# Attention inside a two-layer streaming encoder: two heads' value products issued together on the two column halves of the array, a mask added by strips, new keys kept in the middle of each cache block, and the query latent normalised step by step

## The chip, the core and the metric

The kernel runs on one core of one Trainium2 chip. A core has a matrix engine (PE, with its weight loads listed as PEld), a vector engine (DVE), a scalar or activation engine (ACT), a general engine (POOL) and a queue engine that issues transfers (SP). The metric is the device time of one execution in microseconds (us). Times given for a kernel are medians of the runs shown; the profile is one execution more.

## The reference, cut to what matters

One inference step of an encoder with two trunk layers. Layer 0 mixes a gated linear recurrence with a gated linear attention; layer 1 is a multi-head latent attention (16 heads); each is followed by a SwiGLU feed-forward. There are 256 prompt positions and 8 running streams of 16 new positions each, so 384 columns in all. The change lies in layer 1:

```python
cq, ckv, kpe = split(u @ w_in, [384, 640])
q = (rms_norm(cq, q_norm) @ w_uq).reshape(B, L, 16, 96)      # 64 plain + 32 rotary
# prompt: keys and values are expanded from ckv, block-causal mask over chunks of 64
s = (q_nope @ k_nope + q_pe @ kpe) * SM_SCALE
s = where(key_chunk <= q_chunk, s, -inf);  o = softmax(s) @ v
# samples: 512 cached latents and 16 new ones for each stream
c_all = concat([cache_ckv, ckv]);  k_all = concat([cache_kpe, kpe])
s = (q_lat @ c_all + q_pe @ k_all) * SM_SCALE
o_lat = softmax(s) @ c_all;  o = o_lat @ w_uv
```

All inputs and outputs are float32.

## The kernel before

Activations lie transposed: features on the 128 partitions, the 384 positions (256 prompt, 8 x 16 sample) along the free axis. Most products are made of three matmuls on operands split into a high and a low part (`mm3`, L287 to L289); the parts are of a rounded 32-bit type, with one matmul instruction each. Products of plain float32 operands appear in the trace as two passes, so two PE instructions for one call. Transposes are one pass.

Weights and the samples' caches come as a stream of chunks of 128 x 1024 floats (the caches' transposed chunks, `cT`, have 1056 columns). Each is loaded (L98), copied to a high part on ACT (L110), and its low part is made on DVE (L126) and partly on POOL (L121). The order of the work is the order of the code: the schedule is written out by hand, every engine takes its instructions in order, and waits are set where data needs them.

PSUM (the banks that matmuls write) is dealt out as two rings: six banks `mm` and two `sd`, each given out in turn. A matmul into a bank waits until the previous content has been read.

Layer 1 has four stretches:

- *Query latent.* Six tiles of `cq`, `kpe`, `ckv` come out of one group of matmuls into the six `mm` banks. For each of the three `cq` tiles in turn: DVE scales it (L1129), ACT squares it for the norm (L327, L333, L335), ACT makes the high part with the gain (L311), and DVE makes the low part (L312). Then three heads' queries are computed (the `uq` group, L287 to L289, 27 matmuls, into the first three `mm` banks again), the sums of squares are made (L342, L344) and turned into the two factors (L348, L350), and a matmul with `sel` gathers the rotary key (L1165, in an `sd` bank). The squares of `ckv` (first L327, in the same accumulator tile as those of `cq`) stand ahead of the queries in ACT's order. The normalised `ckv` (L1171) is split into `ckr`, which the values' matmuls read (L297 to L299).
- *Prompt attention.* A loop over ticks t = -1 to 19. In a tick stand, in this order: keys of a pair of heads (odd ticks, `a_keys`), one head's queries (most ticks), the transposes of head t-2 (`a_trans`, L1231), the division of head t-1 (`a_norm`), the value product of head t-3 (`a_value`, L1238 to L1240), the scores of head t (`a_score`). In `a_score` a matmul of the identity with the mask (L1209, 384 columns) opens the sum, and the query-key products follow (L1210, L1211). `a_value` has three products of 128 columns with a stationary tile of 64 columns; even heads write partitions 0 to 63 and odd heads 64 to 127 of a shared bank, in different ticks. After the odd head the pair is copied out (L1243, L1244). In the last ticks, units of the samples' latent queries (L1264, L1401) stand beside it.
- *Sample attention.* A loop over the 8 streams, with the softmax of one beside the products of the one before. Keys are 512 cached ones and 16 new ones, which stand after the cached ones for even streams and ahead of them for odd ones. For stream b the scores of two head groups come in two halves of 264 columns (L1325 to L1328). The probabilities are transposed: four transposes for each group (`trans`, L1353), and in `trans_rest` the 32 columns around the new keys, by a matmul with a stationary tile of 32 columns that writes 32 partitions (L1362). `value` multiplies with the cached latents (four tiles, L287 to L289) and, last, with the new ones: only the 32 partitions `r` that hold the pair of streams, in both operands (shape 32*128), twice in each stream (`ct` = 0 and 1). The rotary keys' cache is loaded by L1284 and split by L1299 (ACT) and L1300 (POOL).
- *Latent to output, output projection, feed-forward*, not touched.

Of the kernel before, what the change touches and what calls it, by code (L numbers as in the profile page):

```python
# [176 lines left out]
def emit(ctx, tc, A, O):  # L177
# [1021 lines left out]
    pair = {}  # L1199
# [7 lines left out]
    def a_score(h, ps):  # L1207
        q, k = qp[:, h % NQ, :], kst[:, h % 4, :]
        pe.matmul(ps, idr, amr, start=True, stop=False)  # L1209
        pe.matmul(ps[:, 0:P], q[:, 0:P], k[:, 0:P], start=False, stop=False)  # L1210
        pe.matmul(ps[:, P:T], q[:, P:TP], k, start=False, stop=True)  # L1211
        mx = small([P, 3], "mx")
        v_.reduce_max(mx, ps.rearrange("p (a b) -> p a b", b=P), axis=AX.X)
        v_.tensor_max(mx[:, 1:2], mx[:, 1:2], mx[:, 2:3])
        v_.tensor_scalar(mx[:, 0:2], mx[:, 0:2], -SM_SCALE, None, op0=OP.mult)
        pr = prb[:, h % 4, :]
        l = small([P, 2], "sl")
        s_.activation(pr[:, 0:P], ps[:, 0:P], AF.Exp, scale=SM_SCALE, bias=mx[:, 0:1], accum_out=l[:, 0:1])
        s_.activation(pr[:, P:T], ps[:, P:T], AF.Exp, scale=SM_SCALE, bias=mx[:, 1:2], accum_out=l[:, 1:2])
        return l  # L1220
# [13 lines left out]
    def a_value(h):  # L1234
        e, pt = h % 2, ptb[:, h % 4, :]
        ps = pair[h // 2][64 * e:64 * e + 64]
        va, vb = vp[0][:, h * 64:h * 64 + 64], vp[1][:, h * 64:h * 64 + 64]
        pe.matmul(ps[:, 0:P], va, pt[:, 0:P], start=True, stop=True)  # L1238
        pe.matmul(ps[:, P:TP], va, pt[:, P:TP], start=True, stop=False)
        pe.matmul(ps[:, P:TP], vb, pt[:, TP:T], start=False, stop=True)  # L1240
        if e:
            hi, lo = oh_at(h // 2), ol_at(h // 2)
            s_.activation(hi[:, 0:TP], pair[h // 2], AF.Copy)  # L1243
            v_.tensor_sub(lo[:, 0:TP], pair.pop(h // 2), f(hi)[:, 0:TP])  # L1244
# [26 lines left out]
    HK = NKEY // 2  # L1271
    HALF = 512

# [3 lines left out]
    def new_at(b):  # L1277
        return slice(0, NS) if b % 2 else slice(PAST, NKEY)

    def past_at(b):  # L1280
        return slice(NS, NKEY) if b % 2 else slice(0, PAST)

    def b_load(b):
        nc.sync.dma_start(krb[b % 2][:, past_at(b)], A["ckpe"][b])  # L1284

    def b_new(b):
        ns = slice(TP + b * NS, TP + (b + 1) * NS)
        c = N_W1 + max(2 * b - 1, 0)
        if c in S.raw:
            pairs = [(S.raw[c], ckv)]  # L1290
        else:
            pairs = [(x, f(ckr)[:, p_]) for p_, x in enumerate(S.parts[c])]
        for x, src in pairs:
            g_.tensor_copy(x.rearrange("p (c k) -> p c k", c=2)[:, :, new_at(b)], src[:, :, ns])
        g_.tensor_copy(krb[b % 2][:, new_at(b)], kper[0:96, ns])
# [6 lines left out]
    class Sample:  # L1302
# [4 lines left out]
        def __init__(self, b):  # L1307
            self.b, self.sc, self.mx, self.l = b, {}, {}, {}
            self.pr = [tmp([P, NS + NKEY]) for _ in range(2)]
            z = 0 if b % 2 else NKEY  # L1310
            for pr in self.pr:
                g_.memset(pr[:, z:z + NS], 0.0)

        def score(self, hg, hi, lo, between=None):
# [3 lines left out]
            self.sc[hg] = [mm(HK) for _ in range(2)]  # L1318
            for e, sc in enumerate(self.sc[hg]):
                if e and between:  # L1320
                    between()
                es = slice(e * HK, (e + 1) * HK)
# [13 lines left out]
        def soft(self, hg):  # L1336
            mx, l, pr = self.mx[hg], small([P, 2], "sls"), self.pr[hg]
            o = NS * (self.b % 2)
            for e in range(2):
                s_.activation(pr[:, o + e * HK:o + (e + 1) * HK], self.sc[hg][e], AF.Exp, scale=SM_SCALE,  # L1340
                              bias=mx[:, 0:1], accum_out=l[:, e:e + 1])
            self.l[hg] = l
# [14 lines left out]
        def trans_rest(self):  # L1357
            self.trans(1)
            r, c0 = rows(self.b), PAST * (1 - self.b % 2)
# [6 lines left out]
        def value(self, hi, lo):  # L1366
            r = rows(self.b)
            self.o = mm(512).rearrange("p (c t) -> p c t", c=2)
            ch, cl = (x.rearrange("p (k c) -> p k c", c=256) for x in (hi, lo))
            for ct in range(2):  # L1370
# [4 lines left out]
                x = tuple(z[r, 4].rearrange("p h t -> p (h t)") for z in (pt_hi, pt_lo))  # L1375
                mm3(self.o[:, ct], (cnew[0][r, cs], cnew[1][r, cs]), x, False, True)
# [35 lines left out]
    for t in range(-1, H_C + 4):  # L1412
        if t % 2:
            if t + 1 < H_C:
                a_keys((t + 1) // 2, mm(TP))
            pair[(t - 3) // 2] = mm(TP)
# [12 lines left out]
        if 0 <= t - 3 < H_C:  # L1429
            a_value(t - 3)  # L1430
# [39 lines left out]
    pt_lo = slot(2, [P, 5, 2, P], F32R, name="pt_lo")  # L1470
    prev = None
# [76 lines left out]
def _pack(inputs):  # L1548
# [67 lines left out]
    ct[0::2, ..., :PAST], ct[1::2, ..., NS:] = cp[0::2], cp[1::2]  # L1616
# [82 lines left out]
```

## Time and profile before

| | |
|---|---|
| median of 3 runs | 1168.84 us (1166.83 to 1172.54) |
| the profiled execution, its time | 1170.78 us |
| the profiled execution, first to last instruction | 1169.0 us |
| busy PE | 1122.6 us (96%), 6627 instructions |
| busy DVE | 673.2 us (58%) |
| busy ACT | 541.8 us (46%) |
| busy POOL | 216.9 us (19%) |
| mean granted TensorE clock | 0.982 of full |

Shares of busy time are means over stages with different limits. A matmul record lasts longer than the time until the next one can start, since matmuls are pipelined; what a matmul costs in a dense stretch is the distance from its start to the next start. A row of the timeline that ends in x4 holds four instructions in a row; brackets give the idle time of the engine ahead of it and what ended it.

### The profile page before, as it was taken

The numbers are of one execution on the slowest core, as the hardware profiler recorded it, in microseconds if no ns is written. First come the engines' busy times: TensorE is split into PE (matmuls) and PEld (weight loads), VectorE is DVE, ScalarE is ACT, GpSimd is POOL, SyncE is SP. The second block draws the span as 40 slices with busy tenths as digits, with TensorE's granted clock in tenths as the row PEclk, the third lists the DMA queues.
The fourth block names the chain that finished last, engine by engine and source line by source line (L and its number), as shares of the span: only waits on it lengthen the run. The fifth ranks groups of instructions, "written<-read, shape, count | busy, mean of one in ns | idle before, by whom it ended". The sixth has DMA issues, their size and how long they took to land.

```text
span 1169.0 us, 16900 instructions
## 1 busy us (share of the span) xinstructions
PE 1122.6 (96%) x6627; PEld 1079.9 (92%) x6627; DVE 673.2 (58%) x1046; ACT 541.8 (46%) x924; POOL 216.9 (19%) x248
## 2 busy tenths in 40 slices
PE   8976999999999999999999899899999999999995
PEld 8976888999999999999999798699899999999995
DVE  5779666856447655553225677677437655554223
ACT  5534485255445433333334566567555433333331
POOL 4178253100112000000102121155212000000102
PEclk9988899999999999999999999999999999999998
DMA  7312247534433333443433251334333433333331
GB/s 260 110 55 66 80 144 241 175 106 168 127 93 122 129 127 127 126 127 126 125 128 98 90 163 55 110 113 134 98 109 108 139 123 124 124 125 124 126 108 54
DMA packets 41745, 142.80 MB, mean 122 GB/s; under 512 B 4833, under 2 KB 7137, under 8 KB 41665
## 3 DMA queue, kind: packets, MB, share of 16 engines
q1 hardware_dynamic: 39744, 135.92, 36.3%
q0 software_dynamic: 1488, 5.31, 1.1%
q8 instruction: 52, 0.85, 0.3%
q10 hardware_dynamic: 432, 0.49, 0.1%
q14 instruction: 29, 0.23, 0.1%
HBM read 134.82 MB, written 6.88 MB: 121 GB/s over the span
## 4 chain that ended last, share of the span: by engine, by line
PE 88%; DVE 7%; ACT 2%; issue 1%; POOL 1%; DMA 1%; SPq 0%; DVEq 0%; ACTq 0%
PE mm L287 25%; PE mm L289 24%; PE mm L288 24%; DVE xc L695 2%; PE mm L297 1%; PE mm L299 1%; PE mm L298 1%; DVE wlo L126 1%; PE sd L530 1%; PE mm L1325 1%; PE mm L1326 1%; PE mm L1327 1%; PE mm L877 1%; PE sd L1353 1%; DMA wraw<-wst 1%
## 5 line engine op out<-in xcount | busy, mean ns | idle before, releaser
L126 DVE TENSOR_TENSOR wlo<-wraw,whi 128x1024 fp32r<-128x1024 f32 (+1 forms) x232 | 278.2, 1200 | 285.8 <-ACT whi L110 285.6
L110 ACT ACTIVATE whi<-wraw 128x1024 fp32r<-128x1024 f32 (+1 forms) x232 | 244.4, 1054 | 232.2 <-PE mm L289 207.7
L287 PE MATMUL mm<-uhi,whi 128*128 128x384 f32 x1016 | 347.2, 342 | 4.2 <-ACT uhi L311 4.1
L289 PE MATMUL mm<-ulo,whi 128*128 128x384 f32 x1016 | 345.3, 340 | 0.8 <-DVE ulo L312 0.8
L288 PE MATMUL mm<-uhi,wlo 128*128 128x384 f32 x1016 | 344.3, 339 | 0.6 <-DVE wlo L126 0.6
L287 PEld LDWEIGHTS mm<-uhi,whi 128*128 128x128 f32 x1016 | 193.0, 190 | 5.5 <-ACT uhi L311 5.0
L289 PEld LDWEIGHTS mm<-ulo,whi 128*128 128x128 f32 x1016 | 192.2, 189 | 1.9 <-DVE ulo L312 1.9
L288 PEld LDWEIGHTS mm<-uhi,wlo 128*128 128x128 f32 x1016 | 192.1, 189 | 1.2 <-DVE wlo L126 1.1
L336 POOL TENSOR_TENSOR acc<-acc,sq 128x384 f32<-128x384 f32 x49 | 59.9, 1222 | 683.1 <-ACT sq L335 682.5
L287 PE MATMUL mm<-ah,whi 128*128 128x384 f32 x352 | 118.9, 338 | 0.0
L289 PE MATMUL mm<-al,whi 128*128 128x384 f32 x352 | 118.9, 338 | 0.0
L288 PE MATMUL mm<-ah,wlo 128*128 128x384 f32 x352 | 118.6, 337 | 0.0
L287 PEld LDWEIGHTS mm<-ah,whi 128*128 128x128 f32 x352 | 66.3, 188 | 0.0
L289 PEld LDWEIGHTS mm<-al,whi 128*128 128x128 f32 x352 | 66.1, 188 | 0.0
L288 PEld LDWEIGHTS mm<-ah,wlo 128*128 128x128 f32 x352 | 66.0, 187 | 0.0
L315 ACT ACTIVATE ah<-tmp 128x384 fp32r<-128x384 f32 x44 | 23.1, 525 | 73.6 <-DVE tmp L1075 73.6
L1071 ACT ACTIVATE tmp<-tmp 128x384 f32<-128x384 f32 x44 | 22.9, 525 | 71.9 <-DVE tmp L1070 71.8
L1072 DVE TENSOR_TENSOR tmp<-mm,r 128x384 f32<-128x384 f32 x44 | 24.5, 556 | 46.9 <-PE mm L289 46.9
L121 POOL TENSOR_TENSOR wlo<-wraw,whi 128x512 fp32r<-128x512 f32 x22 | 32.0, 1455 | 83.0 <-ACT whi L110 73.3
L316 DVE TENSOR_TENSOR al<-tmp,ah 128x384 fp32r<-128x384 f32 x44 | 24.6, 559 | 26.1 <-ACT ah L315 26.1
L695 DVE SCALAR_TENSOR_TENSOR xc<-xp,vec,xc 128x256 f32<-128x256 f32 (+1 forms) x48 | 32.5, 742 | 7.7 <-ACT xc L692 7.7
L335 ACT ACTIVATE sq<-mm 128x384 f32<-128x384 f32 x24 | 11.9, 494 | 38.7 <-PE mm L289 38.6
(351 smaller groups left out, 1842.5 us busy)
## 6 DMA issues: line engine op xcount, KB each, us to landing
wraw<-wst SPq DMA_DIRECT2D x214, 512.0 KB, 3.5
wraw<-cT SPq DMA_DIRECT2D x8, 528.0 KB, 3.6
S<-S SPq DMA_DIRECT2D x8, 512.0 KB, 4.2
o_sS<-S POOLq DMA_DIRECT2D x8, 512.0 KB, 5.5
wraw<-cN SPq DMA_DIRECT2D x8, 512.0 KB, 3.7
h<-x SPq DMA_DIRECT2D x2, 768.0 KB, 5.7
wuk<-wukT SPq DMA_DIRECT2D x2, 768.0 KB, 6.8
x<-x SPq DMA_DIRECT2D x3, 384.0 KB, 7.2
```

Source lines behind the costliest of these rows:

```text
L110: self.nc.scalar.activation(hi[:, s], raw[:, s], AF.Copy)
L121: self.nc.gpsimd.tensor_sub(*(x[:, n:] for x in a))
L126: self.nc.vector.tensor_sub(*a)
L287: pe.matmul(out, wl[0], xr[0], start=start, stop=False)
L288: pe.matmul(out, wl[1], xr[0], start=False, stop=False)
L289: pe.matmul(out, wl[0], xr[1], start=False, stop=stop)
L315: s_.activation(hi, src, AF.Copy)
L316: v_.tensor_sub(lo, src, f(hi))
L336: g_.tensor_add(self.acc, self.acc, q)
L695: v_.scalar_tensor_tensor(dst, src(w), vc("conv_w", 8 * w + c), dst, op0=OP.mult, op1=OP.add)
L1071: s_.activation(z, z, AF.Silu)
L1072: v_.tensor_mul(w, pu, r)
```

## The change

- *Query latent.* The three `cq` tiles are made step by step: all three scalings (each with its high part), then all three low parts, then all three squares. The `sel` matmul goes ahead of the factors and takes an `mm` bank.
- *Mask.* The matmul of the mask comes last in the scores, and only on the columns where the mask is not zero in some row: two strips of 64.
- *Value product.* Both heads of a pair in one even tick, t-4 and t-3: for each head one product of 256 columns with the first value tile and one of 128 columns with the second. The two heads write the two halves of one bank. The loop ends one tick sooner.
- *New keys.* The 16 new keys stand in the middle of the block, between the two halves of 256 cached ones, for every stream. The scores' two parts are of 272 and 256 columns (swapped for odd streams). The rest is transposed by two full transposes, so that the new keys' probabilities land on the right partitions of 128; the tile for them (`pt_hi[:, 4]`, `pt_lo[:, 4]`) is cleared at first and, for streams 2, 4 and 6, on the partitions of the pair before; the last product in `value` takes all 128 partitions. The rotary cache is loaded in two pieces for each row.

```diff
     for i in range(3):
         v_.tensor_mul(cq[:, i, :], pss[i], r2)
+        s_.activation(cqh[:, i, :], cq[:, i, :], AF.Copy, scale=vc("q_norm", i))
+    for i in range(3):
+        v_.scalar_tensor_tensor(cql[:, i, :], cq[:, i, :], vc("q_norm", i), f(cqh)[:, i, :],
+                                op0=OP.mult, op1=OP.subtract)
+    for i in range(3):
         sq_q.add(cq[:, i, :])
-        split_scaled(cqh[:, i, :], cql[:, i, :], cq[:, i, :], vc("q_norm", i))
...
     pss = proj_group([("uq", h) for h in range(3)], cqk, range(3))
+    ps = mm()
+    pe.matmul(ps, sel, kt_, start=True, stop=True)
     fq = sq_q.factor(384)
     rk = sq_k.factor(256)
-    ps = sd()
-    pe.matmul(ps, sel, kt_, start=True, stop=True)
...
+    def strips(t):
+        return bass.AP(tensor=t.tensor, offset=t.offset + 64, ap=[list(t.ap[0]), [TP, 2], [1, 64]])
...
-        pe.matmul(ps, idr, amr, start=True, stop=False)
-        pe.matmul(ps[:, 0:P], q[:, 0:P], k[:, 0:P], start=False, stop=False)
-        pe.matmul(ps[:, P:T], q[:, P:TP], k, start=False, stop=True)
+        pe.matmul(ps[:, 0:P], q[:, 0:P], k[:, 0:P], start=True, stop=False)
+        pe.matmul(ps[:, P:T], q[:, P:TP], k, start=False, stop=False)
+        pe.matmul(strips(ps), idr, strips(amr), start=False, stop=True)
...
-    def a_value(h):
-        e, pt = h % 2, ptb[:, h % 4, :]
-        ps = pair[h // 2][64 * e:64 * e + 64]
-        va, vb = vp[0][:, h * 64:h * 64 + 64], vp[1][:, h * 64:h * 64 + 64]
-        pe.matmul(ps[:, 0:P], va, pt[:, 0:P], start=True, stop=True)
-        pe.matmul(ps[:, P:TP], va, pt[:, P:TP], start=True, stop=False)
-        pe.matmul(ps[:, P:TP], vb, pt[:, TP:T], start=False, stop=True)
...
+    def a_value(hp, ps):
+        args = []
+        for e in range(2):
+            h = 2 * hp + e
+            o, pt = ps[64 * e:64 * e + 64], ptb[:, h % 4, :]
+            args.append((o, pt, *(vp[j][:, h * 64:h * 64 + 64] for j in range(2))))
+        for o, pt, va, vb in args:
+            pe.matmul(o[:, 0:TP], va, pt[:, 0:TP], start=True, stop=False)
+        for o, pt, va, vb in args:
+            pe.matmul(o[:, P:TP], vb, pt[:, TP:T], start=False, stop=True)
...
-        nc.sync.dma_start(krb[b % 2][:, past_at(b)], A["ckpe"][b])
+        nc.sync.dma_start(sides_of(krb[b % 2]), A["ckpe"][b].rearrange("p (e k) -> p e k", e=2))
...
-            ps, c0 = sd([P, 4, P]), 32 * (self.b % 2)
+            ps = sd([P, 4, P])
             for kt in range(4):
-                pe.transpose(ps[:, kt], self.pr[hg][:, c0 + kt * P:c0 + (kt + 1) * P], ident)
+                c0 = kt * P + 32 * (kt // 2)
+                pe.transpose(ps[:, kt], self.pr[hg][:, c0:c0 + P], ident)
...
             for hg in range(2):
-                pe.matmul(ps[r, hg], self.pr[hg][:, c0:c0 + 32], ident, start=True, stop=True)
+                pe.transpose(ps[:, hg], self.pr[hg][:, c0:c0 + P], ident)
+            if self.b and self.b % 2 == 0:
+                for t in (pt_hi, pt_lo):
+                    g_.memset(f(t)[rows(self.b - 1), 4], 0.0)
...
-                x = tuple(z[r, 4].rearrange("p h t -> p (h t)") for z in (pt_hi, pt_lo))
-                mm3(self.o[:, ct], (cnew[0][r, cs], cnew[1][r, cs]), x, False, True)
+                x = tuple(z[:, 4].rearrange("p h t -> p (h t)") for z in (pt_hi, pt_lo))
+                mm3(self.o[:, ct], (cnew[0][:, cs], cnew[1][:, cs]), x, False, True)
...
-    for t in range(-1, H_C + 4):
+    for t in range(-1, H_C + 3):
...
-        if 0 <= t - 3 < H_C:
-            a_value(t - 3)
+        if t % 2 == 0 and 0 <= t - 4 < H_C:
+            a_value((t - 4) // 2, mm(TP))
...
+    for t in (pt_hi, pt_lo):
+        g_.memset(f(t)[:, 4], 0.0)
```

## Rows read from the trace of the kernel before

**Rows 1.** Busy time by stretch (prompt attention, first stream, streams): us, engines, clock, transfers
```profile
682.00:733.00 51.00, 51.00 (x333) 45.66 (x333) 37.34 (x118) 31.48 (x98) 8.16 (x9) 1.00 0.36 108
745.00:763.00 18.00, 13.88 (x88) 11.55 (x87) 12.70 (x27) 10.03 (x24) 6.11 (x14) 0.91 0.14 42
763.00:825.00 62.00, 62.00 (x465) 55.88 (x465) 47.07 (x113) 43.90 (x113) 31.26 (x41) 1.00 0.41 128
```

**Rows 2.** Timeline of PE in two ticks: start, length, engine, line
```profile
684.95 0.34 PE L1209 MATMUL mm<-amr,idr 128*128 128x384 f32 x1
...
701.14 0.49 PE L1231 MATMUL sd<-ident,pr 128*128 128x128 f32 x3
...
701.83 0.38 PE L1239 MATMUL mm<-pt,vp 128*64 128x128 f32 x2
702.04 0.38 PE L1240 MATMUL mm<-pt,vp 128*64 128x128 f32 x2
702.36 0.45 PE L1209 MATMUL mm<-amr,idr 128*128 128x384 f32 x1
702.64 0.38 PE L1210 MATMUL mm<-keys,qp 128*128 128x128 f32 x2
```

**Rows 3.** Timeline of PE: narrow stationary tiles, and rounded matmuls of 128 columns
```profile
167.15 1.06 PE L877 MATMUL mm<-S,qe 128*32 128x256 f32 x8
...
676.37 0.27 PE L299 MATMUL mm<-whi,ckr 128*128 128x128 f32 x1
676.48 0.28 PE L297 MATMUL mm<-whi,ckr 128*128 128x128 f32 x1
...
832.77 2.19 PE L1520 MATMUL mm<-olat,wuv 128*64 128x128 f32 x36
```

**Rows 4.** Timeline of PE around the product with the new latents
```profile
773.83 0.28 PE L289 MATMUL mm<-pt_lo,whi 128*128 128x256 f32 x1
...
774.18 0.28 PE L289 MATMUL mm<-pt_lo,whi 128*128 128x256 f32 x1
774.39 0.38 PE L287 MATMUL mm<-pt_hi,cnh 32*128 32x256 f32 x1
...
775.28 0.28 PE L289 MATMUL mm<-pt_lo,whi 128*128 128x256 f32 x1
```

**Rows 5.** Timeline of PE around the rest's transposes
```profile
778.46 0.60 PE L1353 MATMUL sd<-ident,tmp 128*128 128x128 f32 x4
778.99 0.62 PE L1362 MATMUL mm<-ident,tmp 128*32 128x128 f32 x4
779.54 0.39 PE L1325 MATMUL mm<-whi,ql 128*128 128x264 f32 x1
```

**Rows 6.** Timeline of the query latent, all engines
```profile
655.21 0.56 DVE L1129 TENSOR_TENSOR cq<-mm,r 128x384 f32<-128x384 f32 x1 [1.31 <-ACT r L350]
...
656.95 0.44 PE L287 MATMUL mm<-cqh,whi 128*128 128x384 f32 x1
...
660.04 0.54 DVE L1129 TENSOR_TENSOR cq<-mm,r 128x384 f32<-128x384 f32 x1
...
660.63 0.44 PE L287 MATMUL mm<-cqh,whi 128*128 128x384 f32 x1 [1.78 <-DVE cq L1129]
...
664.42 0.81 PE L342 MATMUL sd<-acc,ones 128*128 128x384 f32 x2
...
665.26 0.52 ACT L327 ACTIVATE acc<-ckv 128x384 f32<-128x384 f32 x1 [3.62 <-PE sd L342]
...
672.62 0.19 PEld L297 LDWEIGHTS mm<-whi,ckr 128*128 128x128 f32 x1 [0.26 <-ACT ckr L315]
```

**Rows 7.** Rotary cache of the streams: landing (us, last figure), issue, first use
```profile
kr<-ckpe SPq DMA_DIRECT2D x2, 192.0 KB, 3.9
...
783.66 0.42 SPq L1284 DMA_DIRECT2D kr<-ckpe  x1
...
790.52 0.63 ACT L1299 ACTIVATE kpb<-kr 96x528 fp32r<-96x528 f32 x1
```

More of the change, by code (lines that the diff above doesn't have):

```diff
@@ L1232, in a_trans @@
         s_.activation(ptb[:, h % 4, :], ps, AF.Copy)
-    def a_value(h):
-        e, pt = h % 2, ptb[:, h % 4, :]
-        ps = pair[h // 2][64 * e:64 * e + 64]
-        va, vb = vp[0][:, h * 64:h * 64 + 64], vp[1][:, h * 64:h * 64 + 64]
-        pe.matmul(ps[:, 0:P], va, pt[:, 0:P], start=True, stop=True)
-        pe.matmul(ps[:, P:TP], va, pt[:, P:TP], start=True, stop=False)
-        pe.matmul(ps[:, P:TP], vb, pt[:, TP:T], start=False, stop=True)
[L1241 to L1244, printed above, removed]
+    def a_value(hp, ps):
[8 more added lines that the diff above has]
+            pe.matmul(o[:, P:TP], vb, pt[:, TP:T], start=False, stop=True)
+        hi, lo = oh_at(hp), ol_at(hp)
+        s_.activation(hi[:, 0:TP], ps, AF.Copy)
+        v_.tensor_sub(lo[:, 0:TP], ps, f(hi)[:, 0:TP])
     tables("exp_and_others")
@@ L1270, in emit, with sides_of @@
     krb = [ckv_s[0:96, 2 * T:2 * T + NKEY], cp.tile([96, NKEY], F32, name="kr1", tag="kr1", bufs=1)]
-    HK = NKEY // 2
+    MID = PAST // 2
     HALF = 512
+    NEW = slice(MID, MID + NS)
     def rows(b):
         return slice(32 * (b // 2), 32 * (b // 2) + 32)
[L1277 to L1281, printed above, removed]
+    def sides_of(t):
+        return bass.AP(tensor=t.tensor, offset=t.offset, ap=[list(t.ap[0]), [MID + NS, 2], [1, MID]])
     def b_load(b):
-        nc.sync.dma_start(krb[b % 2][:, past_at(b)], A["ckpe"][b])
+        nc.sync.dma_start(sides_of(krb[b % 2]), A["ckpe"][b].rearrange("p (e k) -> p e k", e=2))
     def b_new(b):
@@ L1293, in b_new @@
         for x, src in pairs:
-            g_.tensor_copy(x.rearrange("p (c k) -> p c k", c=2)[:, :, new_at(b)], src[:, :, ns])
-        g_.tensor_copy(krb[b % 2][:, new_at(b)], kper[0:96, ns])
+            g_.tensor_copy(x.rearrange("p (c k) -> p c k", c=2)[:, :, NEW], src[:, :, ns])
+        g_.tensor_copy(krb[b % 2][:, NEW], kper[0:96, ns])
     def b_keys(b):
@@ L1309, in __init__ @@
             self.pr = [tmp([P, NS + NKEY]) for _ in range(2)]
-            z = 0 if b % 2 else NKEY
+            self.cut = MID + NS * (1 - b % 2)
+            z = self.cut
             for pr in self.pr:
@@ L1317, in score @@
             ks = [x.rearrange("p (c k) -> p c k", c=2) for x in (hi, lo)]
-            self.sc[hg] = [mm(HK) for _ in range(2)]
+            self.sc[hg] = [mm(n) for n in (self.cut, NKEY - self.cut)]
             for e, sc in enumerate(self.sc[hg]):
@@ L1321, in score @@
                     between()
-                es = slice(e * HK, (e + 1) * HK)
+                es = slice(self.cut, NKEY) if e else slice(0, self.cut)
                 for ct in range(2):
@@ L1337, in soft @@
             mx, l, pr = self.mx[hg], small([P, 2], "sls"), self.pr[hg]
-            o = NS * (self.b % 2)
-            for e in range(2):
-                s_.activation(pr[:, o + e * HK:o + (e + 1) * HK], self.sc[hg][e], AF.Exp, scale=SM_SCALE,
+            for e, es in enumerate((slice(0, self.cut), slice(self.cut + NS, NS + NKEY))):
+                s_.activation(pr[:, es], self.sc[hg][e], AF.Exp, scale=SM_SCALE,
                               bias=mx[:, 0:1], accum_out=l[:, e:e + 1])
@@ L1358, in trans_rest @@
             self.trans(1)
-            r, c0 = rows(self.b), PAST * (1 - self.b % 2)
+            r = rows(self.b)
+            c0 = MID - r.start
             ps = mm(256).rearrange("p (h t) -> p h t", h=2)
             for hg in range(2):
-                pe.matmul(ps[r, hg], self.pr[hg][:, c0:c0 + 32], ident, start=True, stop=True)
+                pe.transpose(ps[:, hg], self.pr[hg][:, c0:c0 + P], ident)
+            if self.b and self.b % 2 == 0:
+                for t in (pt_hi, pt_lo):
+                    g_.memset(f(t)[rows(self.b - 1), 4], 0.0)
             s_.activation(pt_hi[r, 4], ps[r], AF.Copy)
@@ L1366, in value @@
         def value(self, hi, lo):
-            r = rows(self.b)
             self.o = mm(512).rearrange("p (c t) -> p c t", c=2)
@@ L1415, in emit @@
                 a_keys((t + 1) // 2, mm(TP))
-            pair[(t - 3) // 2] = mm(TP)
         ps = mm(512)
```

3 lines of the change are left out of this document (1 added, 2 removed).

## The prediction

> **What bounds the kernel now.** I read the busy time by stretch first, then the timeline of PE in each stretch that the change touches, always from the start of one matmul to the start of the next. In the prompt attention PE is busy 51.00 of 51 us and in the streams 62.00 of 62, while DVE is at 73 and 76% and ACT at 62 and 71% [rows 1]. So in these two stretches the end is set by how soon PE can start its next matmul, and a saved PE slot is a saved slot of the whole, as long as DVE and ACT follow. Two places are bound by chains of several engines instead: the query latent, where PE waits for a bank and for the split latents [rows 6], and the first stream (745 to 763 us: PE 13.88 of 18, clock 0.91 [rows 1]).
>
> The price of PE's slots. A pass with 128 columns of plain float32 costs 0.11: L1239's two passes begin at 701.83, L1240's at 702.04 [rows 2]. A full tick shows what a narrow stationary tile costs beside its passes. From the first of three transposes at 701.14 to the third narrow pass at 701.83 are five slots of 0.11, 0.55, but it took 0.69: 0.14 lost on the way in. The last two narrow passes and the way out took 0.32 instead of 0.22: 0.10. The next matmul, the mask, then held the array for 0.28 (702.36 to 702.64); its record is 0.45 long there and 0.34 where no narrow product stands ahead (684.95), so 0.11 of it belongs to the visit too. One visit to the narrow shape costs 0.35 besides its work.
>
> The same for 32 partitions: three matmuls of `value` take 0.35 (773.83 to 774.18), so six cost 0.70; the six from 774.18 to 775.28, three of them in the 32-partition shape, took 1.10 [rows 4]. A visit costs 0.40. For the rest's transposes: four full ones and the way in 0.53 instead of 0.44 (0.09), the four narrow passes and the way out 0.55 instead of 0.44 (0.11), and the next matmul's record is 0.39 long where those of nearly its length are 0.28 (0.11) [rows 4, 5]: a visit costs 0.31.
>
> **The change part by part.** *Value products.* Before: 16 visits of 0.35 and 16 x 6 passes of 0.11. After: 8 visits. For each head there are two passes of 256 columns and two of 128. The price of the first: eight such passes on two parts of the array were done in 1.06 us (L877), which is possible only when two run side by side: four after each other, 0.22 apart, and the last one's own length of about 0.4 [rows 3]. Halves of 64 do the same: 36 passes of L1520 in 2.19 us, 0.06 each instead of 0.11 [rows 3]. So a pair costs 2 x 0.22 + 2 x 0.11 = 0.66 when the halves overlap, and twice that, 1.32, when they do not. I take 0.66. Saved: 8 x 0.35 = 2.8 for the visits, and 16 x 0.66 - 8 x 0.66 = 5.3 for the passes, 8.1 in all (2.8 at the other end). The value product now waits for the transposes of both heads, the later one made in the tick before; queued behind it on PE are that tick's scores, behind its copy on ACT the exponentials. The copy of the odd head had the same distance before, so I add no wait.
>
> *Mask.* 384 rounded columns cost 0.18 (21 matmuls from 660.63 to 664.42 [rows 6]); 128 cost 0.11 (676.37 to 676.48 [rows 3]). 16 x 0.07 = 1.1. The bound below is nothing, if the strips go as two instructions. What the mask hid after a visit, 0.11, now falls on the first score: it is in the visit's price.
>
> *Rest's transposes.* Two transposes (0.22) in place of four narrow passes (0.44), and no visit: 0.22 + 0.31 = 0.53. In the last stream no scores stand between this and the value products, so PE waits for the copies there anyway and I count seven: 3.7.
>
> *New latents' product.* 128 partitions in place of 32 cost nothing in columns; two visits in each of 8 streams go: 16 x 0.40 = 6.4, less 0.3 for the last, which goes out to narrow products in any case, and 0.2 for those that go out to short transposes: 5.9.
>
> *Clears.* POOL gets two clears of 128 x 256 before the streams and six of 32 x 256. No row shows that size. POOL is busy 31.26 of 62 us [rows 1], and the product that needs them is the last of its group; I take nothing. The bound above: if one of the three later ones came as late as a whole POOL queue of a stream (31.26 us for 6.6 streams, 4.7 us), 3 x 4.7 = 14.
>
> *Query latent.* Before, the third of the three banks was free only after the third scaling at 660.04, since low part and copies stood between the scalings (655.21 to 660.04); PE began with it at 660.63 after 1.78 idle [rows 6]. In the new order the three scalings follow each other at about their length, 0.56, and end by 656.9, and the low parts follow by 0.6 each; so the 27 matmuls run from 656.95 without a stop, 27 x 0.18 = 4.9, until 661.8. Then `sel` (two passes of 384 columns like L342's, 0.65) and L342 at 662.5 instead of 664.42. What follows is a chain: ACT waits for L342 (3.62 idle) with the squares of `ckv` and everything behind them, and 8.2 us after L342 PE gets the split latents, which it waits for already (0.26 idle at 672.62) [rows 6]. The chain itself is not shorter, so the gain is L342's shift, 1.9, and not the whole of PE's saved idle. What is late next: PE has 8 passes of the sums (2.6) and 18 query matmuls (3.2) until then, and stands idle for about 8.2 - 5.8 = 2.4. The squares come later than before, but `sel` and the 27 matmuls stand ahead of their reader. Bounds: nothing, if PE is held elsewhere, and 2.7.
>
> Sum: 8.1 + 1.1 + 3.7 + 5.9 + 1.9 = 20.7 us. The first stream's chain starts when PE has done its part, and moves with it. In the stretches that get shorter DVE comes nearer to its limit: of 51 us some 8 go, and its 37.34 are then 87%; of a stream's 9.4 us (62 us for 6.6 streams: 465 PE instructions, 70 in a stream) 1.3 go, and its 7.1 are 88% [rows 1]. I take off 1 us for waits that this brings. The profiled execution took 1170.78 us and would take 1151.1; it stands 1.9 above the median of the runs shown, 1168.84, so the forecast is 1149.1, say 1149, with a range of its own of 1146 to 1152.
>
> **The rivals.** *DVE becomes the bound.* DVE is idle 13.66 us in the prompt attention and 14.93 in the streams [rows 1]. The change wants 8 and 8.6 of these (58% of each). Part of the idle time is not free: the division of a head waits for ACT's exponentials, which wait for DVE's maximum. If 70% of it is such waiting, only 4.1 and 4.5 us can be had, and the time is 8 us longer: 1157. Against it: the pipeline is two ticks deep, and DVE is not what PE waits for anywhere in those stretches. *The halves run in the order of the code.* A head's two passes stand ahead of the other head's. If a matmul may not start before one that was issued earlier, the second head starts with the first one's second pass, 0.22 in: a pair takes 0.22 + 0.66 = 0.88, and 8 x 0.22 = 1.8 of the gain go: 1151. Against it: L877 and L1520 have the same order by code, four passes on one part and then four on the next, and their 1.06 and 2.19 us are those of full overlap [rows 3]. [...] *Other side: the rotary cache comes late.* Its rows now go in two pieces of half the size, so twice as many. It lands 3.9 us after its issue; from issue (783.66) to use (790.52) are 6.86 us [rows 7]. Streams that are 1.3 shorter leave 5.5. Beyond that each us is lost in the six streams whose load falls here: 1149 + 6 x (landing - 5.5). At twice the landing, 7.8, that is 1163; from 9.8 us on it is slower than now by over 0.5% (1174.7). Against it: it is a small load of 192 KB, and transfers are busy 0.41 of the time [rows 1].
>
> **How the numbers follow.** Forecast 0.62, DVE 0.16, halves in order 0.06, clock 0.08, rotary cache or clears late 0.08, of which 0.04 near the old time and 0.03 above it. The range of 8 in 10 takes in forecast, halves, clock and most of the DVE case: 1145 to 1158; below, if a wait that I count on disappears with the new turn of the banks; above, the DVE case. A measurement of this kernel tells about 0.5%, 5.8 us, from no change. The cases below 1163 give faster 0.92, near it same 0.05, slower 0.03.
>
> **What would show it.** Right: 64 PE instructions in place of 96 in the value products, in 8 groups of some 0.66 plus the visit; mask 0.11 to the next start; no 128*32 and 32*128 shapes in the streams, six matmuls of `value` in 0.70 everywhere; L342 near 662.5 and PE idle ahead of L297 by 2 us or more; streams of 8.1 us instead of 9.4. Wrong: PE idle in the ticks released by DVE or ACT; pairs of 0.88 or 1.3; a wait for L1300 or for the clears ahead of the last product of a stream; a stretch at the lower clock near 670 us.

## The result, and the profile after

The changed kernel took 1151.74 us (median of 4 runs, 1149.9 to 1153.97) against 1167.84 (4 runs) before: ratio 0.9868, interval 0.9853 to 0.9883, so 15.4 us (13.7 to 17.2) by the ratio, 16.1 by the medians. Forecast was 1149, range 1145 to 1158: a gain of 19.7. The profiled execution is the fastest of the four: 1149.9 us, span 1148.1, mean granted clock 0.985. It has none of the stretches at a granted clock of 0.50 that most other profiles of nearly the same kernel show behind the query latent and at the start of the streams (below, The clock).

Busy time by stretch of the changed kernel, columns as in [rows 1]; prompt attention, first stream, streams:

```profile
677.00:723.00 46.00, 45.43 (x309) 40.29 (x308) 36.72 (x117) 30.76 (x97) 8.16 (x9) 1.00 0.35 113
733.00:751.00 18.00, 13.84 (x103) 12.15 (x102) 13.43 (x28) 10.29 (x24) 7.25 (x16) 1.00 0.15 45
751.00:802.00 51.00, 50.97 (x426) 50.34 (x425) 45.09 (x108) 40.58 (x106) 30.77 (x46) 1.00 0.47 151
```

DVE now stands at 80 and 88%; PE still looks full. That hides waits of a few tenths of a microsecond, so the stages are read from the start of one marked matmul to the start of another:

| from, to | before | after | difference |
|---|---|---|---|
| first query matmul (L287, `cqh`) to first prompt value product (L297, `ckr`) | 15.68 | 13.73 | -1.95 |
| first prompt score to last value product | 60.98 | 54.37 | -6.61 |
| second group of stream transposes to the last stream's first | 65.65 | 55.95 | -9.70 |
| first matmul of the output projection to the end | 334.11 | 335.13 | +1.02 |

Of the 9.70 about 1.6 us is not the change's: in the profile of before the clock falls at the start of the streams (0.91 over 18 us [rows 1]), and in this profile of after it doesn't (1.00). So the stages give 1.95 + 6.61 + 8.1 = 16.7 us, near the timed 15.4. The last row is left out: nothing in that stretch is changed, and in kernels that share this code it took 334.10 (gap_flush), 334.11 (undo_latent) and 335.23 (undo_value). Ahead of these stages the two profiles differ by 3.7 us, in layer 0, which the change doesn't touch.

**Where the forecast shows.** PE in a tick with a value product, timeline, changed kernel (answers to [rows 2]):

```profile
700.76 0.49 PE L1238 MATMUL sd<-ident,pr 128*128 128x128 f32 x3
701.18 0.65 PE L1249 MATMUL mm<-pt,vp 128*64 128x256 f32 x4
701.67 0.39 PE L1251 MATMUL mm<-pt,vp 128*64 128x128 f32 x4
701.98 0.49 PE L1216 MATMUL mm<-keys,qp 128*128 128x128 f32 x2
702.31 0.60 PE L1217 MATMUL mm<-keys,qp 128*128 128x256 f32 x2
702.56 0.41 PE L1218 MATMUL mm<-amr,idr 128*128 128x128 f32 x1
```

Eight passes of both heads stand between 701.18 and 701.98, 0.80 with the way out of the narrow shape. With 0.09 on the way in and 0.11 in the next matmul (0.33 to the start behind it for two passes), a pair is 1.00: the counted 0.66 and 0.35. Two ticks that took 8.16 us take 7.04: 1.12 saved, where 1.15 was worked out (1.01 for the pair, 0.14 for two masks; 1.12 three times below).

The query latent, timeline, all engines (answers to [rows 6]):

```profile
651.51 1.49 DVE L1129 TENSOR_TENSOR cq<-mm,r 128x384 f32<-128x384 f32 x3 [1.31 <-ACT r L350]
...
658.72 0.81 PE L342 MATMUL sd<-acc,ones 128*128 128x384 f32 x2
...
659.57 0.52 ACT L327 ACTIVATE acc<-ckv 128x384 f32<-128x384 f32 x1 [4.58 <-PE sd L342]
...
666.93 0.33 PE L297 MATMUL mm<-whi,ckr 128*128 128x128 f32 x1 [2.07 <-ACT ckr L315]
```

L342 stands 5.52 us behind the first query matmul (653.20) instead of 7.47 (664.42 less 656.95), the 8.2 us from it to L297 are as before, and PE is idle 2.07 us ahead of L297 (2.4 was forecast).

In the streams there is no narrow shape left: the rest's transposes and the product with the new latents run at the price of their neighbours (answers to [rows 4, 5]):

```profile
775.01 0.28 PE L287 MATMUL mm<-pt_hi,cnh 128*128 128x256 f32 x1
...
775.37 0.28 PE L287 MATMUL mm<-pt_hi,whi 128*128 128x256 f32 x1
...
778.58 0.60 PE L1363 MATMUL sd<-ident,tmp 128*128 128x128 f32 x4
779.02 0.38 PE L1373 MATMUL mm<-ident,tmp 128*128 128x128 f32 x2
779.15 0.37 PE L1335 MATMUL mm<-whi,ql 128*128 128x272 f32 x1
```

The rotary cache, issue and landing in the streams (answers to [rows 7]); twice as many pieces land as soon as before:

```profile
kr<-ckpe SPq DMA_DIRECT2D x3, 192.0 KB, 3.8
ckv<-ckpe SPq DMA_DIRECT2D x2, 192.0 KB, 4.0
...
759.04 0.57 SPq L1293 DMA_DIRECT2D ckv<-ckpe  x1
...
764.81 0.63 ACT L1308 ACTIVATE kpb<-ckv 96x528 fp32r<-96x528 f32 x1
```

**Where it doesn't.** The distances from the first transposes of one tick to those two ticks on, worked out from the starts of L1231 and L1238 (in both kernels the queries are missing in ticks 6 and 11, and end in tick 12):

| ticks | 3, 4 | 5, 6 | 7, 8 | 9, 10 | 11, 12 | 13, 14 | 15, 16 |
|---|---|---|---|---|---|---|---|
| before | 8.16 | 6.60 | 8.16 | 6.59 | 7.48 | 6.95 | 5.26 |
| after | 7.04 | 5.93 | 7.04 | 5.46 | 7.44 | 5.34 | 5.27 |
| saved | 1.12 | 0.67 | 1.12 | 1.13 | 0.04 | 1.61 | -0.01 |

Pairs of full ticks give what was counted; 5 and 6, 11 and 12, 15 and 16 don't. In 13 and 14 0.63 of the 1.61 is a wait of before that is gone (PE ahead of L1401, 733.82). In 15 and 16 PE now waits 0.80 for the load of `wuk` (L1274, 725.87). Tick 12 of the changed kernel, PE and ACT:

```profile
710.61 0.49 PE L1238 MATMUL sd<-ident,pr 128*128 128x128 f32 x3
...
712.46 1.08 ACT L110 ACTIVATE whi<-wraw 128x1056 fp32r<-128x1056 f32 x1
...
713.43 0.77 ACT L1212 ACTIVATE keys<-mm 64x256 f32<-64x256 f32 x2
713.77 0.65 PE L1249 MATMUL mm<-pt,vp 128*64 128x256 f32 x2
714.23 0.49 ACT L1239 ACTIVATE pt<-sd 128x384 f32<-128x384 f32 x1
714.77 0.43 PE L1249 MATMUL mm<-pt,vp 128*64 128x256 f32 x1 [0.36 <-ACT pt L1239]
```

The transposes of tick 11 (710.61) are copied by ACT only at 714.23, behind the high part of a chunk of the cache (L110, 1056 columns) and the copies of two heads' keys. The second head's value product waits for the copy, and the overlap of the halves is lost with it: the pair takes 1.80 instead of 0.80.

In the streams (8.1 to 8.3 us each, 9.35 before) PE waits again in four of them, 0.1 to 0.2 us ahead of the first transposes (they start 0.22 to 0.32 behind the matmul before them, where 0.12 is usual). The chain that they wait for, DVE and POOL, timeline:

```profile
773.26 1.29 POOL L121 TENSOR_TENSOR wlo<-wraw,whi 128x512 fp32r<-128x512 f32 x1 [1.20 <-ACT whi L110]
...
773.80 1.33 DVE L126 TENSOR_TENSOR wlo<-wraw,whi 128x544 fp32r<-128x544 f32 x1
...
774.62 1.69 POOL L1309 TENSOR_TENSOR kpb<-kr,kpb 32x528 fp32r<-32x528 f32 x1
...
775.98 0.35 DVE L1355 TENSOR_TENSOR sls<-sls 128x1 f32<-128x1 f32 x1
...
776.36 0.17 DVE L1356 RECIPROCAL sls<-sls 128x1 f32<-128x1 f32 x1
776.63 0.50 DVE L1357 TENSOR_SCALAR tmp<-tmp,sls 128x544 f32<-128x544 f32 x1
777.16 0.16 DVE L1355 TENSOR_TENSOR sls<-sls 128x1 f32<-128x1 f32 x1
...
777.28 0.63 PE L1363 MATMUL sd<-ident,tmp 128*128 128x128 f32 x4
```

L1357, the first division, ends at 777.13 and PE starts at 777.28. Ahead of it DVE's L1355, one column, takes 0.35 at 775.98 and 0.16 at 777.16; the slow one ends (776.33) with POOL's L1309 (776.31).

### The profile page after: what moved, and what is told of

It reads as the page before. It is cut to its first block, busy times and chain, and to the rows that moved or that the text cites. A ratio compares the mean times of both kernels' runs of the same rounds, so it can differ in the third digit from the quotient of the medians.

```text
span 1148.1 us, 16830 instructions
## 1 busy us (share of the span) xinstructions
PE 1102.7 (96%) x6579; PEld 1069.1 (93%) x6579; DVE 671.5 (58%) x1046; ACT 539.8 (47%) x924; POOL 219.8 (19%) x256
## 4 chain that ended last, share of the span: by engine, by line
PE 84%; DVE 8%; ACT 3%; issue 2%; DMA 1%; POOL 1%; SPq 0%; DVEq 0%; ACTq 0%
PE mm L287 24%; PE mm L288 24%; PE mm L289 24%; DVE xc L695 2%; DVE wlo L126 1%; PE mm L299 1%; PE mm L297 1%; PE mm L298 1%; ACT whi L110 1%; PE sd L530 1%; PE mm L877 1%; DMA wuk<-wukT 1%; DVE X L517 1%; DMA wraw<-wst 1%; PE sd L342 1%
## 5 line engine op out<-in xcount | busy, mean ns | idle before, releaser
L126 DVE TENSOR_TENSOR wlo<-wraw,whi 128x1024 fp32r<-128x1024 f32 (+1 forms) x232 | 278.5, 1202 | 284.7 <-ACT whi L110 284.5
L287 PE MATMUL mm<-uhi,whi 128*128 128x384 f32 x1016 | 349.6, 344 | 3.2 <-ACT uhi L311 3.2
L110 ACT ACTIVATE whi<-wraw 128x1024 fp32r<-128x1024 f32 (+1 forms) x232 | 244.4, 1054 | 228.8 <-PE mm L289 207.8
L287 PEld LDWEIGHTS mm<-uhi,whi 128*128 128x128 f32 x1016 | 193.6, 191 | 4.3 <-ACT uhi L311 4.1
L287 PE MATMUL mm<-ah,whi 128*128 128x384 f32 x352 | 119.7, 340 | 0.0
L287 PEld LDWEIGHTS mm<-ah,whi 128*128 128x128 f32 x352 | 66.2, 188 | 0.0
```

The lines of the kernel that those rows point to most:

```text
L110: self.nc.scalar.activation(hi[:, s], raw[:, s], AF.Copy)
L126: self.nc.vector.tensor_sub(*a)
L287: pe.matmul(out, wl[0], xr[0], start=start, stop=False)
```

## Experiments

Theory: each part gives back the PE slots that were counted, and what is missing is in new waits (ACT and DVE chains in the short ticks, the division in the streams). Rivals: a part is worth less by itself, the halves don't overlap, or DVE sets the pace throughout. Kernels are compared with the changed kernel, by stage and by time.

### One part undone at a time

`undo_value`: the old `a_value(h)` in each tick at t-3, with its bank for a pair. 

> The value products of the prompt attention are made head by head in the old shape again, three passes of 128 columns each, all else as in the changed kernel. Theory (each visit and each pass is a slot of PE, and the part was worth 8.1 us, of which the waits that the changed kernel has at 714.77 and 725.87 us took back 1.0 and 0.8, and the old wait of the rotary product for a bank, 0.63, comes back with the old bank order): the prompt attention grows from 54.4 us (first score to last value product) to about 60, by 5.5, and the time from 1151.7 to about 1157. Rival (the part gave its full 8.1 and it was the mask that gave nothing): 62.5 us in the stage, time 1160. Rival (DVE and ACT set the pace of the attention now): the added slots vanish in PE's waits, the stage grows by 3 us or less.

`undo_product`:

```diff
-                x = tuple(z[:, 4].rearrange("p h t -> p (h t)") for z in (pt_hi, pt_lo))
-                mm3(self.o[:, ct], (cnew[0][:, cs], cnew[1][:, cs]), x, False, True)
+                x = tuple(z[rows(self.b), 4].rearrange("p h t -> p (h t)") for z in (pt_hi, pt_lo))
+                mm3(self.o[:, ct], tuple(z[rows(self.b), cs] for z in cnew), x, False, True)
```

> The last product of each stream takes 32 partitions again, in 8 streams; the clears and the rest stay. Theory (two visits to another shape in each stream, 0.40 each, PE sets the pace but for the 0.2 us that it now waits for the first transposes of each stream): 5.9 us less six times 0.2 that vanish, 4.7; the streams (second to last stream's first transposes) grow from 55.95 to about 60.5 us, the time from 1151.7 to about 1156.4. Rival (the chain of DVE and ACT bounds a stream at 8.1 us whatever PE does): the streams grow by 2 us or less.

`undo_rest`:

```diff
-                pe.transpose(ps[:, hg], self.pr[hg][:, c0:c0 + P], ident)
+                pe.matmul(ps[r, hg], self.pr[hg][:, MID:MID + 32], ident, start=True, stop=True)
```

> The rest's transposes run as matmuls with 32 columns again, all else as in the changed kernel. Theory (two visits and two narrow passes more in each of seven streams, 0.53 each): 3.7 us, less up to 1.2 for PE's waits of 0.2 at the next stream's transposes: the streams grow from 55.95 to about 58.5 to 59.5 us, the time from 1151.7 to about 1154.5. Rival (the chain of DVE and ACT is the bound of a stream, and PE's saving here went into its waits): 56 to 56.8 us, time within 1 us of the changed kernel.

`undo_latent`: `sq_q.add` and `split_scaled` behind each scaling, and `sel` behind the factors, as before the change. 

> Squares, scalings and low parts of the query latent stand tile by tile again, and the product that folds the rotary keys stands behind the factors, all else as in the changed kernel. Theory (the gain is the shift of the second factor's matmul): from the first query matmul to the first prompt value matmul 15.7 us instead of 13.7, the time 1.9 us longer, about 1153.6. Rival (the first query matmul would have started later by the same amount, so that the part only moved PE's idle time): the stage at 13.7 to 14.2 us, no change in the time.

`undo_mask`: the mask first, over all 384 columns. 

> The mask is added first and over all 384 columns again, all else as in the changed kernel. Theory (0.18 instead of 0.11 for each of 16 heads): the prompt attention grows from 54.4 us by 1.1, to 55.5. Rival (the wide mask's passes are hidden where the array comes back from the narrow shape, in 8 of 16 ticks): 0.6. Rival (DVE and ACT set the pace): nothing.

| kernel | time, median (runs) | ratio to before, interval | its stage | less falls of the clock |
|---|---|---|---|---|
| changed | 1151.74 (4) | 0.9868 (0.9853 to 0.9883) | | |
| undo_value | 1158.13 (4) | 0.9922 (0.9907 to 0.9936) | attention +5.76 | +5.8 |
| undo_product | 1158.52 (4) | 0.9916 (0.9892 to 0.994) | streams +7.06 | +3.6 |
| undo_rest | 1155.41 (4) | 0.9899 (0.9884 to 0.9914) | streams +4.59 | +2.9 |
| undo_latent | 1154.16 (4) | 0.9884 (0.9867 to 0.99) | latent +3.50 | +1.8 |
| undo_mask | 1157.92 (1) | | attention +0.48 | +0.5 |

By time alone undo_latent isn't clear of the changed kernel (the intervals overlap), and undo_mask is one run, with some 5 us lost in two falls of the clock outside its stage (0.95 over the 110 us from 655). What these two parts are worth is read from the stages.

Three of these stages hold a stretch at the lower clock that the changed kernel's profile doesn't have: 9 us at 0.62 in undo_product, 5 at 0.66 in undo_rest and 4 at 0.58 in undo_latent. One minus the clock, times the length, is the estimate of what it cost at most: 3.4, 1.7 and 1.7 us. The row of undo_product, by stretch:

```profile
745.00:754.00 9.00, 6.97 (x35) 6.80 (x36) 5.54 (x14) 4.92 (x13) 3.69 (x7) 0.62 0.33 99
```

and that of undo_latent:

```profile
659.00:663.00 4.00, 4.00 (x16) 4.00 (x15) 2.58 (x5) 0.48 (x1) 0.00 (x0) 0.58 0.01 4
```

The period of a stream is free of that. It is 8.21 us in the changed kernel (mean of five), 8.83 in undo_product, 8.61 in undo_rest: 0.62 and 0.40 a stream, 4.3 and 2.8 us in seven. Counted were 0.80 and 0.53 for the two; 0.13 to 0.18 went into the wait ahead of the transposes, which is gone in both: in undo_rest they start 0.12 behind the matmul before them, in undo_product 0.21 behind a narrow product, as before the change, with the division done 0.7 us earlier (783.29, PE 783.99). All five parts are worth something, value products and new latents' product most, in the order of the sum; the rivals that a part gives nothing fall. For the mask the last rival but one comes nearest in size (0.6), for another reason: two full ticks take 7.19 instead of 7.04, so the mask is worth 0.07 in each as counted; ticks that wait hide the rest.

### Do the halves overlap, and in what order?

```diff
-        for o, pt, va, vb in args:
             pe.matmul(o[:, 0:TP], va, pt[:, 0:TP], start=True, stop=False)
-        for o, pt, va, vb in args:
             pe.matmul(o[:, P:TP], vb, pt[:, TP:T], start=False, stop=True)
```

(`code_order`: both lines in one loop.) 

> The four value matmuls of a pair are written head by head (both passes of the first head, then both of the second) in place of pass by pass. Theory (passes on different halves of the array don't wait for each other in the order of the code, as rows of before show): a pair still takes about 0.66 us plus its visit, and the prompt attention stays at 54.4 us within 0.2. Rival (a matmul may not start before the one issued earlier, so the second head starts with the first head's second 128-column pieces or later): 0.22 to 0.66 more a pair, 1.8 to 5.3 us in the stage.

`same_half`: that, and `o = ps[0:64, TP * e:TP * e + TP]` for both heads. 

> Both heads of a pair are put on the same half of the array (partitions 0 to 63, 256 columns apart), head by head; the copy becomes two copies of 64 partitions on ACT, and the low parts of these outputs are left out (a subtraction of the same size that gives zero stands in their place). Theory (half of what the value products gave back comes from two halves at work at once): a pair takes 1.32 us instead of 0.66, the prompt attention grows from 54.4 by about 5.3, less up to 0.7 for the wait at 714.77 us that hides in it: 59.0 to 59.7. Rival (the gain came from fewer visits and wider passes, and the overlap is one of records only): 54.4 to 55 us.

PE in a tick with a pair, code_order:

```profile
700.90 0.66 PE L1249 MATMUL mm<-pt,vp 128*64 128x256 f32 x4
701.38 0.40 PE L1250 MATMUL mm<-pt,vp 128*64 128x128 f32 x4
701.71 0.49 PE L1216 MATMUL mm<-keys,qp 128*128 128x128 f32 x2
```

and same_half:

```profile
711.74 0.65 PE L1249 MATMUL mm<-pt,vp 128*64 128x256 f32 x2
712.22 0.38 PE L1250 MATMUL mm<-pt,vp 128*64 128x128 f32 x2
712.44 0.59 PE L1249 MATMUL mm<-pt,vp 128*64 128x256 f32 x2
712.87 0.38 PE L1250 MATMUL mm<-pt,vp 128*64 128x128 f32 x2
713.18 0.49 PE L1216 MATMUL mm<-keys,qp 128*128 128x128 f32 x2
```

code_order: all four wide passes start before the narrow ones, though half of the narrow ones stand ahead of the second head's wide ones in the code. A pair takes 0.81 to the next score as in the changed kernel, the stage +0.20 (time 1152.84, 1 run). same_half: 1.44, 0.64 more, where 0.66 was counted; the stage grows by 3.88 (time 1158.10, 1 run) and not by 4.6 to 5.3, since the short ticks' waits hide part of it there too: ticks 11 and 12 take 7.19, less than the 7.44 of the changed kernel. So nearly all of the passes' gain (0.64 of 0.66 a pair) is two halves at work at once, whatever the order of the code; wider passes by themselves give next to none of it, and what is left of the part is the visits.

### The new waits

`rope_first`: the first six units in the order latent, latent, rotary, rotary, latent, latent. 

> The sample latents' two units of heads 4 to 7 change places with the rotary unit of these heads, so that the second wuk load is needed one tick later. Theory (at 725.87 us PE waits 0.8 for that load, which lands at 725.83 and lies behind the load of a cache chunk in SP's queue): the wait goes, the stretch from the first latent unit to the last value product shrinks from 13.48 us to about 12.7. Rival (the load is on nobody's path in truth, since the tick's transposes wait for DVE's division at the same time): 13.2 us or more.

 From the first latent unit to the last value product 13.52 us instead of 13.48 (time 1152.76, 1 run): the rival holds. The wait for `wuk` is gone, and PE waits 0.46 and 0.17 for DVE's division (L1232) in the ticks behind it. These ticks have no queries, and the chain from a tick's scores over maximum, exponentials and division to its transposes is as long as they are.

`gap_flush`: `Q_TICKS` without 6 and 10, and the `S.flush()` between `cur.soft(0)` and `cur.top(1)` left out, so that the next `chunk` does it. 

> Two edits in two stages that are read apart. In the prompt attention the ticks without queries are 6 and 10 in place of 6 and 11; in the streams DVE's part of the splitting of the next chunk (1.3 us) stands behind the second maximum and the first division instead of ahead of them. Theory: tick 12's value product no longer waits for the copy of tick 11's transposes, which was late behind a conversion of weights and the copies of keys on ACT, and the tick of 4.76 us goes back to about 4.4 (and the one after it gains or loses little): 0.4 to 1.0 us less in the attention. A stream's division is ready 1.3 us earlier, PE's wait of 0.2 to 0.3 ahead of the first transposes goes, and streams of 8.2 to 8.3 us become 8.0 to 8.1. Rivals: the wait moves to tick 10, where a shorter tick meets the same chain (no gain in the attention); the second division is now late in its turn, and PE waits as long ahead of the second transposes (streams stay at 8.2).

 Time 1156.69, 1 run. Attention: -0.20. Ticks 11, 12 take 6.35 instead of 7.44, 13 to 16 another 0.55 less, and ticks 9, 10 take 6.86 instead of 5.46: the wait moved, as the rival said. The streams went the wrong way, to 9.0 to 9.4 us. DVE and POOL in one of them:

```profile
769.70 1.31 POOL L1309 TENSOR_TENSOR kpb<-ckv,kpb 32x528 fp32r<-32x528 f32 x1
770.06 0.97 DVE L1355 TENSOR_TENSOR sls<-sls 128x1 f32<-128x1 f32 x1 [0.17 <-ACT tmp L1349]
...
771.75 0.72 DVE L126 TENSOR_TENSOR wlo<-wraw,whi 128x544 fp32r<-128x544 f32 x1
772.03 1.58 POOL L121 TENSOR_TENSOR wlo<-wraw,whi 128x512 fp32r<-128x512 f32 x1 [1.02 <-ACT whi L110]
772.39 1.24 DVE L1355 TENSOR_TENSOR sls<-sls 128x1 f32<-128x1 f32 x1
```

Now both divisions' one-column sums (0.16 alone) run beside a POOL instruction and end with it: 771.03 beside 771.01, 773.63 beside 773.61. PE waits 7.6 us in all, up to 1.2 at a time, for L1357. So by these rows the sums wait for POOL and not behind other work of DVE, and with DVE's piece out of the chain both of them fall under POOL's. No run took POOL's pieces away, so that the streams would then be shorter isn't shown.

`warm_share` (with the fill below) moves columns from DVE to POOL at that place: `S.share(736)` instead of `S.share(HALF)`. 

> That kernel, and GpSimd takes 736 instead of 512 columns of each cache chunk's low part behind the scores, so that DVE's piece, which stands ahead of the second maximum and the first division, is 320 columns at most instead of 544. Theory (the chain of DVE sets a stream at 8.2 to 8.3 us, and PE waits 0.2 to 0.3 for the first division): streams of 8.05, 1 us less in the six of them. Rivals (GpSimd's piece grows by 0.5 us and delays the rotary keys behind it, or both engines slow each other down, 1.3 us each for 512 columns now): streams at 8.2 or longer.

```profile
773.11 1.77 POOL L121 TENSOR_TENSOR wlo<-wraw,whi 128x736 fp32r<-128x736 f32 x1 [1.19 <-ACT whi L110]
...
773.66 1.56 DVE L126 TENSOR_TENSOR wlo<-wraw,whi 128x320 fp32r<-128x320 f32 x1
```

The streams took 8.5 us: the rival that the two slow each other. DVE's 320 columns take longer (1.56) than 544 (1.33) did, and POOL's piece beside them ends later (774.88 instead of 774.55); from a stream's first transposes to the end of DVE's piece it is 6.36 us instead of 6.11.

### The clock

Among the prediction's chances the clock has 0.08. In the changed kernel's profile PE is idle 2.07 us ahead of the latents and the clock stays at 1.00 behind it (665 to 676 us). In others it doesn't: of nine profiles with that gap unfilled and of that length, seven show a stretch of 3 to 4 us at a lower clock right behind it (0.50 in its whole microseconds, 0.84 over the 11 us from 665), two (the changed kernel's and undo_product's) don't. Here code_order, 4 us at 0.57:

```profile
667.00:671.00 4.00, 4.00 (x16) 3.42 (x15) 3.81 (x7) 2.46 (x5) 2.69 (x6) 0.57 0.64 228
```

The first prompt score then comes 1.55 us later. At the start of the streams, behind gaps of 1.15, 1.34 and 1.68 us, nine of eleven unfilled profiles show such a stretch (0.93 or 0.86 over the 25 us from 740, so 1.7 or 3.5 us lost at most), before's among them. So PE's gaps were filled:

```diff
+    def busy(ps, n):
+        for _ in range(n):
+            pe.matmul(ps[:, 0:P], ones, ones, start=True, stop=True)
...
+            if hf == ct == 0:
+                busy(vps[0], 18)
             wide(vps, "uv", ct, 4 * hf, ckt(ct), ct == 0, ct == 1)
```

and in the same way ahead of the first stream's second scores (9), the second stream's rotary product (11) and the first stream's second transposes (14). 

> The changed kernel with idle PE time filled by products of ones that nothing reads: 18 of 128 columns (0.11 us each) ahead of the first prompt value product, where PE stands idle 2.07 us, and 9, 11 and 14 in the three gaps of the first streams (1.15, 1.34 and 1.68 us). [...]

 The clock stayed at 1.00 at both places, but the kernel took 1153.11 us (4 runs): the fill was twice as long as meant. The trace shows two passes for each of these plain float32 products, 36 for 18, at 0.11 us each:

```profile
668.38 4.26 PE L1192 MATMUL mm<-ones 128*128 128x128 f32 x36
```

and L297 came 1.95 us late, the first stream's second transposes another 2.7. Then with half of it, 9, 5, 5 and 7. 

> The same fill of PE's idle time with half as many products of ones (9, then 5, 5 and 7), since a plain float32 product takes two passes of 0.11 us and not one: 1.98 us in the gap of 2.07 and 1.1, 1.1 and 1.5 in those of 1.15, 1.34 and 1.68. Theory: no stretch at the lower clock between 660 and 820 us and nothing delayed, so the query latent takes 13.7 us, the first prompt value products up to the first score 9.3 or less, the first stream 13.1 in all as in the changed kernel's profile, and the timed median falls by 1.5 to 3 us against the changed kernel's 1151.7, to 1149 to 1150. Rival (the falls come anyway, or move to the next gap): 1151 to 1153.

 warm_half: 1150.84 us (6 runs, 1148.35 to 1153.39), ratio 0.9842 (0.9817 to 0.9867); warm_share: 1151.12 (4 runs), 0.9847 (0.9822 to 0.9873). In both the clock is 1.00 from 655 to 765 us, and in warm_half nothing there is late. So in three of three filled profiles there is no fall at either place. But warm_half's interval overlaps the changed kernel's: that it is faster is not shown. And its profile has a fall behind the last stream's gaps, as those of code_order and rope_first have; warm_half by stretch:

```profile
807.00:811.00 4.00, 4.00 (x25) 3.91 (x23) 0.33 (x1) 0.00 (x0) 1.46 (x1) 0.67 0.63 211
```

## Why the prediction held, and where it was off

- *Query latent, 1.9:* 1.95 in the stage, 1.8 by undoing it. The step "the gain is L342's shift, and not the whole of PE's saved idle" was right: the idle time moved to L297. The clock, at 0.08 among the chances, weighs more than that: seven of nine profiles have a fall to 0.50 behind this gap, at 1.55 us where it was measured, most of what the part gives; the profile of the changed kernel has none (1.00). What the fall does to the comparison stays open, since the old order's gap of 1.78 us can be followed by the same (undo_latent at 659 us, 0.58 over 4 us; the profile of before not, 1.00). It was given 0.08 as if it were a property of the kernel; it is there in one profile and not in another where the gap is the same 2.07 us.
- *Value products, 8.1:* the prices were right: 1.01 a pair (two full ticks of undo_value take 8.05 against 7.04), the halves overlap (0.80 a pair, 1.44 on one half in same_half), and the rows of L877 and L1520 were a fit guide to it. Undoing it cost the stage 5.8.
- *Mask, 1.1:* 0.07 in a full tick as counted, 0.5 in the stage.
- *Rest's transposes 3.7, new latents' product 5.9:* 2.8 and 4.3 by the periods. Together a stream became 1.14 us shorter (9.35 to 8.21), where 1.33 was counted.
- *The step that was mis-sized* is "I take off 1 us for waits that this brings". It came to about 4: 20.7 less 16.7, 2.6 in the prompt attention (9.2 less 6.6, and that with an old wait of 0.63 gone that wasn't counted) and 1.5 in the streams (9.6 less 8.1). Of the 1.5 the waits ahead of the first transposes are 0.6 (0.10, 0.15, 0.20 and 0.16); 0.5 was counted for the last stream, where nothing was gained (11.01 us from its first transposes to the output projection before, 11.09 after); 0.4 stays open. The step before it, "the copy of the odd head had the same distance before, so I add no wait", is wrong in tick 12: the distance was the same in ticks, but the tick between became 1.06 us shorter (2.68 instead of 3.74), and ACT's copy didn't. And I spread the gain of 1.15 over all pairs of ticks, though some (next to ticks 6 and 11, and from 13 on) lack the queries that give the chains of DVE and ACT their time.
- *DVE becomes the bound:* true of these places only. PE's waits in the streams come from the first division. Ahead of it DVE's L126 took 1.33 us beside POOL's instructions (0.72 where it started ahead of POOL's piece, gap_flush) and its one-column sum 0.35 instead of 0.16: 0.8 us lost beside POOL, and not DVE's load alone.
- *Rotary cache, clears:* no wait of PE for either shows that the kernel before didn't have. The load lands 3.8 to 4.0 us behind its issue, as before, and is needed 5.8 behind it (759.04 to 764.81).
- *Halves in code order:* refuted by code_order: 0.81 us a pair head by head, 0.80 pass by pass, and the second head's wide passes start ahead of the first head's narrow ones (L1249 x4 from 700.90, L1250 x4 from 701.38).

Open: what rules whether a gap is followed by the lower clock; and whether the streams reach 8.05 if POOL's two pieces are placed so that no DVE sum falls under them, or DVE takes the whole low part. Neither was tried.

## What to carry to other kernels

Price a change of PE slots where PE is dense, then look at the sections that lack the usual filler (here the ticks without queries): there the chain of other engines sets the pace and a saved slot can be worth nothing (0.04 and -0.01 us in two pairs of ticks here), so count the gain by sections and not by instructions. Compare single profiles stage by stage and take stretches at the lower clock out first; they were worth as much as a small part of the change (1.7 or 3.4 us at most by the estimate above, where the query latent gave 1.95). Ahead of moving work between DVE and POOL, look at which instructions of the two end together (here 320 columns took DVE 1.56 us beside POOL's longer piece, 544 took 1.33 beside the shorter one).

## What the runs showed of the hardware that was not expected

- DVE's subtraction L126 and one-column sum L1355, where they started while a POOL subtraction ran, ended only behind it: the sum (128x1) took 0.97 and 1.24 us instead of 0.16 (gap_flush) and ended 0.02 us behind POOL both times; 320 columns took 1.56 (warm_share), 544 columns 1.33 (changed kernel, 773.80). The other way round, a DVE piece of 544 columns that started first took 0.72, and POOL's piece beside it 1.58 instead of 1.29 (gap_flush); POOL's L1309 took 1.69 behind a DVE piece (774.62) and 1.31 without one (gap_flush, 769.70). Two maxima of `mm` banks took 0.76 beside POOL's L1309 (775.05) and 0.76 where POOL was idle (799.80).
- Matmuls on the two halves of the array didn't keep the order of the code: with the first head's passes all ahead of the second's, the second head's wide passes started ahead of the first head's narrow ones, a pair in 0.81 us (code_order) against 1.44 on one half (same_half).
- The granted clock fell to 0.50 for 3 to 4 us behind a PE gap of 2.07 us in seven of nine profiles (0.84 over the 11 us from 665), and behind the gaps of 1.15 to 1.68 us at the start of the streams in nine of eleven (0.93 over the 25 us from 740; 0.86 in three of them, where the fall was twice as long); with the gaps filled by products that nobody reads it stayed at 1.00 there in three of three.
